# A dilated convolution on one core: nine rows of a store split over 124 and 4 partitions, and the semaphores cleared before the last transfer has landed

## The chip, the cores and the metric

The kernel runs on one core of one Trainium2 chip. The metric is device time in microseconds (us); several runs of one kernel give a median and a spread. The profile is of one execution, and its times count from the start of that execution's span.

## What is computed

A 3x3 convolution with dilation 2 over 16 images of 64 channels and 64x64 pixels, to 128 output channels, in float32 at both ends. `x_pad` is the image with two zeros on every side:

```python
for b in range(batch):
    for co in range(c_out):
        for ci in range(c_in):
            for kh in range(k):
                for kw in range(k):
                    output[b, co] += weight[co, ci, kh, kw] * x_pad[b, ci, kh*dilation:kh*dilation+h, kw*dilation:kw*dilation+w]
```

The input is 16 x 64 x 64 x 64 x 4 B = 16.8 MB, the output twice that, 33.6 MB.

## The kernel before

The images are worked in 8 pairs. A pair's input lies on 128 partitions (two images of 64 channels), its output on 128 partitions (the output channels) with the two images one after the other along the row: `osb[pb % 3]` has 2 x 4096 float32 in each partition. A pair is cut in four groups of 16 rows (`GR = 16`, `NG = 4`), so there are 32 groups `G`.

For each group ScalarE casts input rows to float16 (line 204), VectorE forms sums of row pairs (line 267), TensorE runs three chains of matmuls (line 224), ScalarE copies the shared product out of PSUM (line 210), and VectorE adds it to the two others into `osb` (line 285). Each of these engines runs its own list in group order and waits on counters (`Count`, a semaphore with its running total).

All transfers are issued by SyncE (SP) on one queue, in an order written out by hand: the weights (line 92), four pairs of input (line 98, called from `load`), and then, pair by pair, a wait for the last add of that pair (`done`, line 299), the stores of its two images (`store`, line 301, which issues at line 303) and, while there are any, loads of later pairs. A transfer adds 16 to its semaphore when it is complete; all stores of pair `pb` count on `s_store[pb]`.

The last pair (`pb = 7`) is stored by halves (lines 331 to 335): when its second group is done, rows 0 to 31 of both images go out; when its fourth is done, rows 32 to 63 of both. Each of these four transfers is 128 partitions x 8192 B (32 rows x 64 columns x 4 B). They are the last four transfers of the program.

GpSimd (POOL) has nothing to do after the start but the end: it waits until every `s_store[pb]` has its full count (line 337) and then clears all semaphores of the kernel with one instruction over their range (line 338). After that come the closing barriers of the program (lines 52 and 369 in the profile).

Of the kernel before, what the change touches and what calls it, by code (L numbers as in the profile page):

```python
# [9 lines left out]
def kernel(  # L10
# [7 lines left out]
    nc = tc.nc  # L18

    B, CI, H, W = x.shape  # L20
# [7 lines left out]
    P = 128  # L28
# [5 lines left out]
    HW = H * W  # L34
    GR = 16
    NG = H // GR
# [6 lines left out]
    OF = 3  # L43
# [6 lines left out]
    out_img = out.rearrange("b o h w -> b o (h w)")  # L50

    ctx.enter_context(tc.tile_critical())  # L52
    pe, act, dve, pool, sp = nc.tensor, nc.scalar, nc.vector, nc.gpsimd, nc.sync

    def sb(name, cols, dt):
        return nc.alloc_sbuf_tensor(name, [P, cols], dt).ap()

    x32 = [sb(f"x32_{i}", HW, f32) for i in range(XF)]
    osb = [sb(f"osb_{i}", 2 * HW, f32) for i in range(OF)]
# [24 lines left out]
    sems = []  # L84
# [2 lines left out]
    s_first, s_sum, s_addA, s_addB = map(Count, ("s_first", "s_sum", "s_addA", "s_addB"))  # L87
    s_load = [Count(f"s_load{pb}") for pb in range(npairs)]
    s_store = [Count(f"s_store{pb}") for pb in range(npairs)]


    s_w.by(sp.dma_start(out=w32, in_=weight.rearrange("o i h w -> o (i h w)")), 16)
# [12 lines left out]
    for pb in range(1, XF):  # L105
# [9 lines left out]
            out=ident,  # L115
            in_=ident,
# [156 lines left out]
    for G in range(ngroups):  # L273
        pb, g = divmod(G, NG)
# [7 lines left out]
        for e, c in ((0, s_addA), (1, s_addB)):  # L282
# [3 lines left out]
                    out=o[:, :, b0 : b0 + NBLK, e],  # L286
# [11 lines left out]
    def done(G):  # L298
        sp.wait_ge(s_addB.s, G + 1)

    def store(pb, m, r0=0, r1=H):
        s_store[pb].by(
            sp.dma_start(
                out=out_img[2 * pb + m, :, r0 * W : r1 * W],
                in_=osb[pb % OF][:, m * HW + r0 * W : m * HW + r1 * W],
            ),
            16,
        )

    def store_both(pb, r0, r1):  # L310
        s_store[pb].by(
# [6 lines left out]

    done(NG - 2)
    store(0, 0, 0, (NG - 1) * GR)  # L320
    store(0, 1, 0, (NG - 1) * GR)
    done(NG - 1)
    store_both(0, (NG - 1) * GR, H)
    more(XF)
    for pb in range(1, npairs - 1):
        if pb + XF < npairs:
            more(pb + XF, (0, H) if pb < 2 else (0, H // 2, H))
        done(NG * pb + NG - 1)
        store(pb, 0)
        store(pb, 1)  # L330
    pb = npairs - 1
    for g in (1, NG - 1):
        done(NG * pb + g)
        store(pb, 0, (g - 1) * GR, (g + 1) * GR)
        store(pb, 1, (g - 1) * GR, (g + 1) * GR)
    for pb in range(npairs):
        pool.wait_ge(s_store[pb].s, s_store[pb].n)
    nc.clear_and_free_semaphores(sems)


# [33 lines left out]
```

## Time and profile before

| | |
|---|---|
| time, median of 3 runs | 129.51 us (128.9 to 129.54) |
| profiled execution, its own time | 128.65 us |
| span of the profiled execution | 126.9 us |
| PE / DVE / ACT / POOL busy, share of the span | 82% / 72% / 51% / 2% |
| packets of the one queue that SP fills (q1), share of 16 engines' span | 95.2% |
| moved | 50.66 MB, mean 399 GB/s |
| HBM read / written | 17.07 MB / 33.55 MB |

The profile lists, for each compute engine, how long it was busy; for the transfers, how much of the 16 DMA engines' time was taken by packets. A packet is one contiguous piece that a DMA engine moves; in this kernel it is the part of one partition's row that a transfer names, or 4 B that count up a semaphore. "Landing" is the moment at which the last of a transfer's increments arrived. A slice in the page's rows of digits is 126.9 / 40 = 3.17 us.

### The profile page before, as it was taken

Reading aid. Unit: us, or ns where it says so; the run is one execution under the profiler, and the core shown is the slowest. Engines: PE = TensorE matmul, PEld = TensorE weight load, DVE = VectorE, ACT = ScalarE, POOL = GpSimd, SP = SyncE. Lnnn points to the kernel's source line nnn. Section 1 sums busy time; section 2 is a strip of 40 time slices with the busy share of each in tenths; the row PEclk is TensorE's granted clock in tenths of the full one; section 3 lists DMA queues with packets and bytes.
Section 4 is the critical chain, followed back from the end, with each engine's and each line's share of the span. In section 5 each row is a group of like instructions: output and inputs, shape, how many; then the busy total and the mean of one; then the engine's idle time right before and its main releaser. Section 6 shows DMA issues by size and latency. Waiting matters only on the chain. (4 is left out here: it accounts for less than half of the span.)

```text
span 126.9 us, 2394 instructions
## 1 busy us (share of the span) xinstructions
PE 104.5 (82%) x1000; PEld 56.6 (45%) x1000; DVE 91.0 (72%) x103; ACT 64.9 (51%) x68; POOL 2.2 (2%) x8
## 2 busy tenths in 40 slices
PE   5849999999999999999999999998999999200000
PEld 2325555555555565555555655553555555000000
DVE  0656888988898888888888988878889887600000
ACT  4366566656665666566656665665466633000000
POOL 2400000000000000000000000000000000000000
PEclk9999999999999999999999999999999999995555
DMA  4999999899999999999999999999999999999930
GB/s 111 375 445 439 424 424 403 320 435 403 444 438 444 413 413 434 418 424 449 416 439 416 449 421 413 447 439 429 413 424 444 444 413 418 449 405 426 429 165 15
DMA packets 4595, 50.66 MB, mean 399 GB/s; under 512 B 496, under 2 KB 496, under 8 KB 1008
## 3 DMA queue, kind: packets, MB, share of 16 engines
q1 hardware_dynamic: 4592, 50.63, 95.2%
q8 instruction: 1, 0.02, 0.0%
q14 instruction: 2, 0.02, 0.0%
HBM read 17.07 MB, written 33.55 MB: 399 GB/s over the span
## 5 line engine op out<-in xcount | busy, mean ns | idle before, releaser
L285 DVE TENSOR_TENSOR osb<-ps,psb 128x1024 f32<-128x1024 f32 x64 | 76.8, 1223 | 13.7 <-PE ps L224 12.5
L224 PE MATMUL ps<-x,w_sb 64*128 64x496 f16 (+3 forms) x768 | 84.4, 365 | 0.6 <-PEq L242 0.6
L224 PEld LDWEIGHTS ps<-x,w_sb 64*128 64x128 f16 x768 | 43.7, 94 | 36.5 <-issue 2.3
L210 ACT COPY psb<-ps 128x1024 f32<-128x1024 f32 x32 | 32.4, 1013 | 37.5 <-PE ps L224 37.5
L204 ACT CAST x<-x 128x1024 f16<-128x1024 f32 (+2 forms) x31 | 32.4, 1046 | 0.0
L224 PE MATMUL ps<-xs,w_sb 64*128 64x496 f16 (+1 forms) x192 | 26.0, 371 | 1.6 <-PEq L242 1.6
L224 PEld LDWEIGHTS ps<-xs,w_sb 64*128 64x128 f16 x192 | 10.9, 94 | 10.3 <-issue 1.9
L267 DVE TENSOR_TENSOR xs<-x 128x512 f16<-128x512 f16 x32 | 13.3, 416 | 0.7 <-ACT x L204 0.7
L133 PE MATMUL ps<-zero 128*128 128x512 f16 x10 | 4.1, 533 | 1.4 <-DVE zero L169 1.4
L171 DVE CAST wd<-w 128x192 f16<-128x192 f32 x1 | 0.5, 503 | 2.6 <-DMA w<-in_weight_dram 2.6
L133 PEld LDWEIGHTS ps<-zero 128*128 128x128 f16 x10 | 1.0, 122 | 2.8 <-DVE zero L169 1.4
L144 PEld LDWEIGHTS ps<-ident,wd 128*64 128x64 f16 x30 | 1.0, 109 | 1.9 <-issue 1.5
L144 PE MATMUL ps<-ident,wd 128*64 128x128 f16 x30 | 1.4, 223 | 0.4 <-DVE wd L171 0.4
L183 ACT ACT_TABLE_LOAD x1 | 1.3, 1283 | 0.9 <-SPq L52 0.9
L183 ACT CAST wd<-w 128x192 f16<-128x192 f32 x1 | 0.5, 542 | 1.7 <-DMA w<-in_weight_dram 1.7
L175 DVE CAST w_sb<-ps 128x384 f16<-128x384 f32 x2 | 1.1, 550 | 0.4 <-PE ps L144 0.4
L185 ACT CAST w_sb<-ps 128x384 f16<-128x384 f32 x1 | 0.5, 480 | 1.3 <-PE ps L144 1.3
L169 DVE MEMSET zero<- 128x256 uint32 x1 | 0.3, 272 | 1.1 <-SPq L52 1.1
L188 ACT CAST x<-x 128x512 f16<-128x512 f32 x1 | 0.6, 620 | 0.8 <-DMA x<-in_x_dram 0.8
L177 DVE CAST x<-x 128x640 f16<-128x640 f32 x1 | 0.5, 493 | 0.5 <-DMA x<-in_x_dram 0.5
L125 POOL TENSOR_TENSOR wd<-w 128x192 f16<-128x192 f32 x1 | 0.8, 794 | 2.3 <-DMA w<-in_weight_dram 2.3
L126 POOL CAST wd<-w 128x192 f16<-128x192 f32 x1 | 0.8, 808 | 0.0
(9 smaller groups left out, 2.7 us busy)
## 6 DMA issues: line engine op xcount, KB each, us to landing
out_dram<-osb SPq DMA_DIRECT2D x12, 2048.0 KB, 19.7
x<-in_x_dram SPq DMA_DIRECT2D x5, 2048.0 KB, 18.3
out_dram<-osb SPq DMA_DIRECT2D x5, 1024.0 KB, 13.9
x<-in_x_dram SPq DMA_DIRECT2D x4, 1024.0 KB, 21.5
out_dram<-osb SPq DMA_DIRECT2D x2, 1536.0 KB, 12.4
x<-in_x_dram SPq DMA_DIRECT2D x1, 1088.0 KB, 5.7
x<-in_x_dram SPq DMA_DIRECT2D x1, 960.0 KB, 7.5
w<-in_weight_dram SPq DMA_DIRECT2D x1, 288.0 KB, 2.9
```

Of the source, the lines that this page charges most:

```text
L125: s_pool.by(pool.tensor_tensor(out=wdv[:, 3], in0=wv[:, 0], in1=wv[:, 1], op=sub))
L126: s_pool.by(pool.tensor_copy(out=wdv[:, 4], in_=wv[:, 2]))
L133: pe.matmul(out=dm[:, 0:512], lhsT=zero[:, 0:P], rhs=zero)
L144: m = pe.matmul(out=ps[r * CI : (r + 1) * CI, j * CO : (j + 1) * CO], lhsT=wd[:, t * CI : (t + 1) * CI], rhs=ident,)
L175: dve.tensor_copy(out=turned(k)[0], in_=turned(k)[1])
L183: s_wda.by(act.copy(out=wdv[:, 2], in_=wv[:, 0]))
L188: cast_n[0] = s_act.by(act.copy(out=x16[:, 0 : 8 * W], in_=x32[0][:, 0 : 8 * W]))
L204: act.copy(out=x16[:, lo * W : hi * W], in_=x32[pb % XF][:, lo * W : hi * W])
L210: copy_n[G] = s_act.by(act.copy(out=psb[G % PF], in_=slot(G, 0)))
L224: m = pe.matmul(out=po, lhsT=w_sb[pp, t * CO : (t + 1) * CO], rhs=rhs, start=first and j == 1, stop=last and j == 2,)
L267: s_sum.by(dve.tensor_tensor(out=s, in0=v[:, :, 0], in1=v[:, :, 1], op=add))
L285: dve.tensor_tensor(out=o[:, :, b0 : b0 + NBLK, e], in0=slot(G, 1 + e).rearrange("p (m b q) -> p m b q", m=2, q=2 * W), in1=pv, op=add,)
```

## The change

Three things are changed, all at the end of the kernel.

The store of the first half (rows 0 to 31) of the last image was one transfer of 128 partitions x 8192 B. It becomes three: rows 0 to 22 over 128 partitions (5888 B in each), rows 23 to 31 over partitions 0 to 123 (2304 B in each), and the same nine rows over partitions 124 to 127 (2304 B in each).

The very last store (rows 32 to 63 of the last image) counts on a semaphore of its own, `s_last`. POOL waits for the other stores and for SP's having issued everything (`s_issued`), clears all semaphores but `s_last`, and only then waits for `s_last`.

The instruction that waits for `s_last` also takes its count back to zero, so that no clearing comes after it.

```diff
+    s_issued = Count("s_issued")
+    s_last = Count("s_last")
...
-    def store(pb, m, r0=0, r1=H):
-        s_store[pb].by(
-            sp.dma_start(
-                out=out_img[2 * pb + m, :, r0 * W : r1 * W],
-                in_=osb[pb % OF][:, m * HW + r0 * W : m * HW + r1 * W],
-            ),
-            16,
-        )
+    def store(pb, m, r0=0, r1=H, rows=((0, P),), c=None):
+        for lo, hi in rows:
+            (c or s_store[pb]).by(
+                sp.dma_start(
+                    out=out_img[2 * pb + m, lo:hi, r0 * W : r1 * W],
+                    in_=osb[pb % OF][lo:hi, m * HW + r0 * W : m * HW + r1 * W],
+                ),
+                16,
+            )
...
-    for g in (1, NG - 1):
-        done(NG * pb + g)
-        store(pb, 0, (g - 1) * GR, (g + 1) * GR)
-        store(pb, 1, (g - 1) * GR, (g + 1) * GR)
+    FOUR = ((0, P - 4), (P - 4, P))
+    ROWS4 = 9
+    done(NG * pb + 1)
+    store(pb, 0, 0, 2 * GR)
+    store(pb, 1, 0, 2 * GR - ROWS4)
+    store(pb, 1, 2 * GR - ROWS4, 2 * GR, FOUR)
+    done(NG * pb + NG - 1)
+    store(pb, 0, 2 * GR, H)
+    store(pb, 1, 2 * GR, H, c=s_last)
+    sp.sem_inc(s_issued.s, 1)
+
+
+    pool.wait_ge(s_issued.s, 1)
     for pb in range(npairs):
         pool.wait_ge(s_store[pb].s, s_store[pb].n)
-    nc.clear_and_free_semaphores(sems)
+    nc.clear_and_free_semaphores(sems[:-1])
+    pool.wait_ge(s_last.s, s_last.n).then_inc(s_last.s, -s_last.n)
+    nc.release_semaphore(s_last.s)
```

## The prediction

> **What bounds the kernel now.** I read the page's rows by slices first, then the chain that ended last, then the transfers from 109 us on, then POOL's last instructions.
>
> The rows by slices (40 slices of 3.17 us; the digit is a busy share in tenths):
>
> ```profile
> PE   5849999999999999999999999998999999200000
> DVE  0656888988898888888888988878889887600000
> DMA  4999999899999999999999999999999999999930
> ```
>
> The 16 DMA engines are full from the second slice on. Compute stops five slices before the end. The chain of waits, in order of time, ends with VectorE:
>
> ```profile
> 107.54 2.36 DVE osb L285 x2
> ```
>
> That is 109.90 us; the span is 126.88. What follows is no engine's work: the stores still queued. SP issues the last two at once:
>
> ```profile
> 109.92 1.48 SPq L303 DMA_DIRECT2D out_dram<-osb  x2
> ```
>
> The transfers between 109 and 127 us (40 slices of 0.45 us):
>
> ```profile
> DMA  9959968999899999999999999996311111000000
> GB/s 583 401 255 510 583 255 364 419 437 455 364 473 419 419 437 419 401 455 419 419 437 437 419 419 437 400 473 255 127 55 55 55 55 55 18 18 0 0 0 0
> ```
>
> This row carries the prediction. About 420 GB/s until some 121.5 us, then 55, then 18, then nothing. Stretches, with the DMA share and GB/s as the last two numbers:
>
> ```profile
> 118.00:120.00 2.00, 0.00 (x0) 0.00 (x0) 0.00 (x0) 0.00 (x0) 0.00 (x0) 0.50 1.02 430
> 122.70:124.40 1.70, 0.00 (x0) 0.00 (x0) 0.00 (x0) 0.00 (x0) 0.00 (x0) 0.50 0.11 48
> 124.46:125.10 0.64, 0.00 (x0) 0.00 (x0) 0.00 (x0) 0.00 (x0) 0.00 (x0) 0.50 0.06 26
> ```
>
> With all at work 430 / 16 = 26.9 GB/s each; alone, one moves 26. So a DMA engine's pace is its own and doesn't rise when the others stop. And 26 GB/s is one engine: two of the sixteen work alone at the end, then one. In the trace's packet records the last increments of fourteen engines go out between 121.34 and 122.24 us, of the other two at 124.45 and 125.13. **The end is set by two late DMA engines**, up to 125.13 - 122.24 = 2.89 us behind the last of the rest. Each had the same bytes: all transfers here have 128 partitions, 8 for each engine.
>
> Then POOL (durations min/median/max in ns, then first and last start):
>
> ```profile
> L338 POOLq DRAIN  x1: 105/105/105, 125.7 to 125.7; - x1
> L338 POOLq EVENT_SEMAPHORE_RANGE_CLEAR  x1: 200/200/200, 125.8 to 125.8; - x1
> L52 POOLq DRAIN  x1: 34/34/34, 126.1 to 126.1; - x1
> ```
>
> The last increment lands at 125.57 (15.3 us after the issue at 110.30), 0.45 after its packet. In the records POOL's wait follows at 125.598, the drain at 125.684, the clearing at 125.819, the closing drain at 126.068; the span ends at 126.88.
>
> **Part 1, the nine rows.** They are 9 x 64 x 4 = 2304 B in each partition. Before, they were part of a packet of 8192 B, 8 packets per engine. In the packet records consecutive packets start 306 ns apart at 8192 B, 156 at 4096 (stores), 288 at 7680 and 90 at 2304 (the weights); 8192 and 2304 make 36.7 ps per byte and 5.5 ns per packet, so 5888 B take 221 ns.
>
> For twelve engines: 8 x (306 - 221) = 0.68 us less, if they have no share of the nine rows. For those that take them: how a transfer of 124 partitions is divided no row shows. All traced transfers give every engine equal shares; 124 doesn't divide by 16, and the largest count up to 16 that divides both 124 and 4 is four. So I take four engines with 31 packets from one transfer and 1 from the other. Such an engine: 8 x 221 + 32 x 90 + 2 increments of 6 = 4.66 us, against 8 x 306 = 2.45: 2.21 us more. The bounds: packets 86 ns each by the pace alone (2304 / 26.8; 0.13 us less in all), or slower from sharing (rival 2); shares of one sixteenth (nothing changes) or all on four.
>
> If the four are among the fourteen, they finish between 121.34 + 2.21 = 123.55 and 122.24 + 2.21 = 124.45. The late ones finish at 123.77 and 125.13 - 0.68 = 124.45. So the late one still ends, or is level: **0.68 us gained**, and no more rows would help.
>
> The Trainium skill, "DMA: Bandwidth & Descriptors", section "Why a DMA increments its semaphore by 16 and not by 1", says that the number of engines is the largest up to 16 that divides the slowest dimension, and that SP's queue uses the lowest-numbered; "Latency and other measured facts" there calls engines 7 and 15 usually the slower ones. Together they would make the four miss the late ones. The trace's two late engines fit this; which numbers they have no record here shows.
>
> SP issues two transfers more. Its issues took 0.33 to 1.11 us; after the pair at 103.6 to 105.05 it waits until 109.92, so 2 x 1.11 fits in its 4.9 us. If it didn't, the last pair would be issued later, with engines that have work until 114.3 and beyond (the first landing of the pair issued at 103.6). Cost nothing.
>
> **Part 2, the clearing.** Drain and clearing go from behind the last landing to before it: the closing drain can start where the drain did, 126.068 - 125.684 = **0.38 us gained**. Bounds: 0.31 if the closing drain then takes the other's 105 ns instead of 34, 0.40 if the wait is faster (17 instead of 43 ns). Cover: POOL now waits for the last store but one, which an engine ends 2.45 us before its last, and the clearing needs some 0.5; uncovered it would cost those 0.38 back. SP's signal comes with its last issue, 111.4 us in this trace, 11 us before it is needed. Behind POOL's new wait stands only the closing drain. The decrement is in the waiting instruction; a wait with a decrement took 17 ns in the closing barrier.
>
> **Sum.** 0.68 + 0.38 = 1.06 us. Against the profiled execution: 128.65 - 1.06 = 127.59. The median of the runs shown is 0.86 above that execution, so the prediction is 129.51 - 1.06 = 128.45, 0.8% faster. An unprofiled lag may differ; that the runs are longer than the profiled one speaks against a smaller one, since the other fourteen had no idle time to lose.
>
> **Rivals.** *1: the move relieves nobody.* The nine rows may be shared out nearly evenly after all, or the late engine's pace may hang on the partitions it reads and not on the engine, so that others that read them take its time away. Then only the clearing counts: 129.51 - 0.38 = 129.13, no change that a measurement of this kernel can tell (0.5%, 0.65 us). For it: no traced transfer lets an engine read another's partitions. Against it: the pace stayed at 26 GB/s with one engine alone.
>
> *2: the four become the end, slower than before.* The place is their 32 packets. They have 124.45 + x against 125.13 + 0.38 of the old end, so it is slower from x = 1.06 us for the last of them, 33 ns on each packet (from 1.96 us, 61 ns, if the four are the earliest). If a packet takes twice as long, because it meets another engine that reads the same partitions, x = 32 x 90 = 2.88: the end is at 126.43 to 127.33, 1.30 to 2.20 later, less 0.38 gives 130.43 to 131.33. If one of the two late engines is among the four, it ends at 124.45 + 2.21 or 125.13 + 2.21, which with the 0.38 gives 130.66 to 131.34. For it: the first 2304 B packets of the weights took up to 642 ns while all began at once. Against: later ones held 93.
>
> A rule speaks for this rival: the skill's "SBUF — State Buffer", section "Door 1: The DMA port swizzle", has 16 ports, each for eight fixed partitions, and DMA speed limited by the ports reached. By it 31 neighbouring partitions read by one engine use ports that are already full, and the sum would be near rival 2 instead of -1.06. No row of before can show it.
>
> **How the numbers follow.** If any four of the sixteen are as likely, they miss both late ones with 12/16 x 11/15 = 0.55. I give the forecast 0.56 and divide the rest evenly: rival 1 0.22, rival 2 0.22. The forecast's own range is 127.7 (lowest run 128.9 less 1.06, rounded down) to 128.8 (less 0.68, where the lag is 0.4 short). Over 0.5% faster: 0.56, within: 0.22, slower: 0.22. The range goes from 127.6 to the near end of rival 2, 130.4; what lies beyond has under 0.2.
>
> **What would show it.** In the profile after: the tail at 48 to 55 GB/s replaced by about 100 to 160 (four to six engines), ending near 124.5 instead of 125.1; landing of the last transfer near 124.9; 31 packets of 2304 B on each of four engines, 90 ns apart; POOL's clearing near 123 and the closing drain some 0.1 us after the last landing. Packets of 2304 B well over 93 ns, or four engines that end after 125.1, would be rival 2; a tail as before, rival 1. The prediction is wrong if the late engines of the timed runs are others, or less late.

## The result, and the profile after

| | before | after |
|---|---|---|
| median of 19 runs | 128.78 us (128.12 to 130.22) | 127.71 us (127.40 to 129.44) |
| profiled execution / its span | 128.65 / 126.9 us | 127.42 / 125.6 us |
| last landing in that profile | 125.57 us | 124.71 us |
| from there to the end of the span | 1.31 us | 0.93 us |

The ratio after to before is 0.9927, 95% interval 0.9904 to 0.9949: 0.94 us faster, by the interval 0.66 to 1.24. The three runs of before that the prediction was made against lay high: their median was 129.51, that of 19 runs is 128.78.

The page of the kernel after, first its span, then the row of the DMA engines by slices of 3.14 us, then SP's queue (packets, MB, share of 16 engines' span):

```profile
span 125.6 us, 2398 instructions
...
DMA  3999999899999999999999999999999999999971
...
q1 hardware_dynamic: 4728, 50.63, 96.4%
```

The row ends in 71 instead of 30: the engines now stop more nearly together. There are 136 packets more than before: 128 of 2304 B and 8 increments. The transfers from 109 to 127 us, in slices of 0.45 us as for before:

```profile
DMA  9798989999999999999999998966444320000000
GB/s 510 328 546 364 473 346 382 401 455 419 400 411 394 431 395 467 395 428 449 418 415 462 392 497 364 492 291 255 200 182 200 146 109 36 0 0 0 0 0 0
```

The 55 and 18 GB/s of two engines and then one have become about 200, some seven engines (the four with the nine rows and, in this execution, three late ones), and 36 in the last slice. The drop from full speed comes half a slice to a slice earlier and the end earlier too: the rest is spread over more engines.

POOL's last instructions (durations in ns, then first and last start):

```profile
L350 POOLq DRAIN  x1: 105/105/105, 122.4 to 122.4; - x1
L350 POOLq EVENT_SEMAPHORE_RANGE_CLEAR  x1: 201/201/201, 122.5 to 122.5; - x1
```
```profile
L351 POOLq EVENT_SEMAPHORE  x1: 17/17/17, 124.7 to 124.7; - x1
```
```profile
L52 POOLq DRAIN  x1: 34/34/34, 124.8 to 124.8; - x1
```

Drain and clearing are over at 122.71, two microseconds before the last landing. Behind the wait for it (L351) comes the closing drain at once, at 124.83.

SP's four issues of the first halves, in place of two:

```profile
L306 SPq DMA_DIRECT2D out_dram<-osb x4: 332/1061/1112, 103.8 to 106.4; - x4
```

The last of them ends at 107.54 (106.44 + 1.10); SP's next issue is at 110.12, after the last add as before (109.92 there).

In the packet records the pieces of 2304 B follow each other every 90 ns on four engines (each took 93 ns and overlaps the next by 3), those of 5888 B every 221. The landings of the very last transfer are 121.32 to 122.14 for nine engines, then 123.51, 123.86, 124.12, 124.21, 124.33, 124.57 and 124.71. Which is which follows from the second transfer of the pair before, whose parts landed at 111.87 to 113.03, and late at 114.35, 115.06 and 115.20. From there an engine without the nine rows has 24 packets of 8192 B, 8 of 5888 and four increments: 24 x 0.306 + 8 x 0.221 + 4 x 0.006 = 9.14 us. So the late ones land at 123.49, 124.20 and 124.34 (found: 123.51, 124.21, 124.33). With 32 x 0.090 + 2 x 0.006 more, 12.03 us, the four are the ones at 123.86, 124.12, 124.57 and 124.71 (from 111.87, 112.14, 112.57 and 112.71: 123.90, 124.17, 124.60, 124.74). In this execution **the four end last, 0.38 us behind the late ones.**

The last landing is 0.86 us earlier than in before's profile, but not all of that is the change. The latest part of the pair before had landed at 115.20 here and at 115.79 there, so the late engine was 0.59 us less late to begin with. With the store in one, 32 packets of 8192 B and four increments follow: 32 x 0.306 + 4 x 0.006 = 9.82 us, which gives before's last landing to 0.04 (115.79 + 9.82 = 125.61, found 125.57). Here it would have been 115.20 + 9.82 = 125.02, so by this estimate the nine rows took 0.31 us off the last landing in this execution.

### The profile page after: what moved, and what is told of

It is laid out like the page before. It is cut to its first block, busy times and chain, and to the rows that moved or that the text cites. A ratio compares the mean times of both kernels' runs of the same rounds, so it can differ in the third digit from the quotient of the medians.

```text
span 125.6 us, 2398 instructions
## 1 busy us (share of the span) xinstructions
PE 104.5 (83%) x1000; PEld 55.9 (44%) x1000; DVE 91.0 (72%) x103; ACT 64.9 (52%) x68; POOL 2.2 (2%) x8
## 5 line engine op out<-in xcount | busy, mean ns | idle before, releaser
L226 PEld LDWEIGHTS ps<-x,w_sb 64*128 64x128 f16 x768 | 43.2, 94 | 36.8 <-issue 2.1
```

The source lines that it names most:

```text
L226: m = pe.matmul(out=po, lhsT=w_sb[pp, t * CO : (t + 1) * CO], rhs=rhs, start=first and j == 1, stop=last and j == 2,)
```

## The experiments

All are edits of the kernel after, or of before where it says so; ratios are to before, and 0.01 is 1.29 us.

**The two parts alone.** First the nine rows with the old end:

```diff
...
-    store(pb, 1, 2 * GR, H, c=s_last)
-    sp.sem_inc(s_issued.s, 1)
+    store(pb, 1, 2 * GR, H)
...
-    pool.wait_ge(s_issued.s, 1)
...
-    nc.clear_and_free_semaphores(sems[:-1])
-    pool.wait_ge(s_last.s, s_last.n).then_inc(s_last.s, -s_last.n)
-    nc.release_semaphore(s_last.s)
+    nc.clear_and_free_semaphores(sems)
```

> The nine rows over 124 and 4 partitions alone; the clearing stays behind the last landing as before. If the late DMA engines are relieved by 8 packets of 85 ns, the last transfer lands 0.6 to 0.7 us earlier and the kernel is that much faster, about -0.65 us. If the move relieves nobody, no change. If the clearing alone made the gain, no change either. The two parts are independent if this and the clearing alone add up to the whole change (about -0.94 us by the ratio 0.9927).

Measured: 0.9933 (0.9907 to 0.9959), 0.86 us faster, by the interval 0.53 to 1.20. The transfers from 109 to 127 us in its profile:

```profile
DMA  7998989899999998999999999955433312000000
GB/s 328 473 510 364 401 364 492 364 419 419 435 399 402 444 444 362 463 410 433 438 410 431 410 419 401 401 219 218 182 164 164 164 73 91 18 0 0 0 0 0
```

The last landing is at 125.32, and the span ends 1.31 us later, as before. In this execution the latest engine was later: its part of the pair before landed at 116.23. With the store in one it would have landed 9.82 us on, at 126.05; with the rows moved it is 9.14, 125.37. So by this estimate the move took 0.73 us off, and here the late engine ends last, at 18 GB/s, with the four done by 124.80 (112.81 + 12.03 = 124.84 for the last of them). The move relieves the late engines. Then the earlier clearing with the store in one:

```diff
-    store(pb, 1, 0, 2 * GR - ROWS4)
-    store(pb, 1, 2 * GR - ROWS4, 2 * GR, FOUR)
+    store(pb, 1, 0, 2 * GR)
```

> The earlier clearing alone; the store of the first half stays one transfer. From the last landing to the end of the span 1.31 us before and 0.93 in the changed kernel, so -0.38 us here (ratio 0.997) and the last landing where it was. If the gain of the change is all in the clearing, -0.9 us.

Measured: 0.9959 (0.9928 to 0.9989), 0.53 us faster, by the interval 0.14 to 0.93; the expected 0.38 lies in it. In its profile the last landing is at 125.52 (before: 125.57), and the wait's instruction and the closing drain follow at 125.54 and 125.64. The transfers from 109 to 127 us still end with two engines and one:

```profile
DMA  9969996999999999999998999995311010000000
GB/s 510 510 291 437 473 382 273 473 401 455 419 437 419 455 400 473 401 437 437 382 492 346 437 419 437 419 455 219 146 55 73 36 73 18 36 0 0 0 0 0
```

So both parts bring something. Whether either alone is the whole can't be told by time: 0.53 to 1.20 and 0.14 to 0.93 both overlap the 0.66 to 1.24 of the change. The profiles show that each does its own part: with the rows alone the 1.31 us behind the last landing are back, with the clearing alone the last landing is where it was.

**The same pieces, over all engines.**

```diff
-    store(pb, 1, 2 * GR - ROWS4, 2 * GR, FOUR)
+    store(pb, 1, 2 * GR - ROWS4, 2 * GR)
```

> As the changed kernel, but the nine rows are one transfer over all 128 partitions, so every engine has 8 packets of 2304 B and the bytes are even again. If what helps is which engines take the nine rows, this is the clearing alone, -0.35 us, with two late engines alone at the end. If cutting the store into smaller pieces helps by itself, it is as fast as the changed kernel, -0.94 us.

Measured: 0.9983 (0.9953 to 1.0013), 0.2 us faster, which can't be told from none; the clearing's 0.38 lies in the interval, the 0.94 of the change doesn't. Its tail is that of before, down to the single engine's 18 GB/s:

```profile
DMA  9969977997999998999999998989321111000000
GB/s 473 437 291 546 473 328 328 473 437 309 505 397 436 395 423 355 498 405 463 403 387 494 374 509 346 492 346 382 127 91 73 73 55 55 18 0 0 0 0 0
```

Cutting the store up isn't what helps; which engines move the pieces is.

**Seven engines.** An attempt to spread more rows over more engines:

```diff
-    FOUR = ((0, P - 4), (P - 4, P))
-    ROWS4 = 9
+    FOUR = ((0, 119), (119, 126), (126, P))
+    ROWS4 = 16
```

> As the changed kernel, but sixteen rows instead of nine, over 119, 7 and 2 partitions. If a transfer goes to as many engines as the largest count up to 16 that divides its partitions, always the first ones, the sixteen rows (4096 B, 156 ns) go to seven engines with 17 or 18 packets (one or two engines 19) instead of 8. Those seven end 1.4 to 1.6 us later than before, at 122.9 to 123.8; the late ones have 8 x 150 = 1.2 us less and end near 123.9 instead of 125.1: -1.2 us from the transfers and -0.38 from the clearing, -1.6 us in all. If the seven include a late engine, that one ends near 126 and the kernel is slower than before by 0.5 us or more. If engines that read others' partitions are slowed, packets of 4096 B take well over 159 ns.

Measured: 1.0179 (1.0128 to 1.0230), slower by 2.3 us. One engine alone ends at 128.2, more than three microseconds after the others (a stretch of that time; DMA share and GB/s are the last numbers):

```profile
125.80:128.20 2.40, 0.00 (x0) 0.00 (x0) 0.00 (x0) 0.00 (x0) 0.00 (x0) 0.50 0.06 24
```

A late engine is among the seven. And packets were stretched, which the changed kernel didn't show: of the pieces of 4096 B, 159 ns alone, sixteen took 13 to 632 ns longer, the last two of these (632 and 329 ns, at 121.01 and 121.87) at a time when only the late engine can still have had pieces. 18 or 19 pieces more (2.8 to 3.0 us), 8 packets shorter by 150 ns (1.2 us less) and those 0.96 us make 2.6 to 2.8 of the 3.1 us by which it ends later than the last one of before (128.2 against 125.1).

**Eighteen rows.**

```diff
-    ROWS4 = 9
+    ROWS4 = 18
```

> As the changed kernel with eighteen rows instead of nine over 124 and 4 partitions. 18 rows are 4608 B, 175 ns a packet at the changed kernel's pace; the four engines have 32 of them and 8 packets of 3584 B (137 ns) in place of 8 of 8192 B: 6.7 us instead of 2.45, 4.2 us more. They end near 126.4 and the last landing is near 126.8, 1.3 us later than before; with the clearing's -0.38 the kernel is about 0.9 us slower than before (ratio 1.007). If engines that read other engines' partitions also slow each other, the packets take well over 175 ns and it is slower still. If the nine rows helped in another way than by the balance of bytes, eighteen help as much or more: -0.9 us or better.

Measured: 1.0201 (1.0123 to 1.0280), slower by 2.6 us where 0.9 was expected; the last landing is at 127.85 instead of 126.8. In the packet records 18 of the 128 pieces of 4608 B took 11 to 391 ns longer than the 178 ns of the others, 3.6 us in all, and 18 packets of 8192 B another 1.7 us. The tail falls in long steps, four engines that end one after the other:

```profile
DMA  9999969999999999999899997434343333222120
GB/s 510 400 437 401 510 291 401 419 400 455 388 413 395 428 465 386 456 386 482 351 411 379 412 353 270 165 137 181 142 174 146 164 127 127 109 91 109 73 91 36
```

So there is a point from which the four are the end, and beyond it a second price: packets that take longer. What lengthens them isn't shown.

**Which engines are late.** The kernel before, with row 63 of the second image of two pairs in pieces, each with a semaphore of its own:

```diff
+    PIECES = {5: (4, 5, 6, 7, 8, 9, 10, 15, 64), 6: (11, 12, 13, 14, 14, 64)}
...
         store(pb, 0)
-        store(pb, 1)
+        if pb in PIECES:
+            store(pb, 1, 0, H - 1)
+            lo = 0
+            for n in PIECES[pb]:
+                marker(pb, lo, lo + n)
+                lo += n
+        else:
+            store(pb, 1)
```

> The kernel before, with row 63 of the second image of the sixth and seventh pair stored in pieces of 4, 5, 6, 7, 8, 9, 10, 15 and of 11, 12, 13, 14 partitions, each with its own semaphore; nothing is left out. Each engine does its queue in order, so an engine that is 2 to 3 us late lands its part of each piece 2 to 3 us late. If a piece of n partitions goes to the first n engines, always the same ones, the number of late landings in a piece of n tells how many late engines are among the first n: 0 for 4 by the changed kernel, 1 for 7 by the run with seven engines (its last landing was 3.4 us behind the others). If late engines are the eighth and the last, as the notes on the chip would have it, there is none up to 7 and one from 8 to 15. The time itself is of no interest here; some us more are expected from twelve small issues.

The increments of each piece, by time in us. Here are four of the pieces. One update comes as SP's issue ends, 10 to 15 us before the others (left of the bar), and then there is one for each engine:

```
 4:  86.70 | 101.98 102.17 102.61 103.02
 5:  87.58 | 102.18 102.35 102.79 103.21 105.68
11: 100.41 | 111.80 111.96 111.97 112.19 112.37 112.39 112.57 112.66 113.11 113.58 116.37
12: 101.54 | 111.99 112.14 112.15 112.40 112.58 112.61 112.76 112.84 113.30 113.77 115.17 116.57
```

A piece of n partitions lands n times, for each of the n from 4 to 15. From 4 to 5 one landing is added that is 2.5 us late, so **the fifth engine is late**, if a piece of n goes to the first n engines, always the same ones; up to 11 there is no other, and the twelfth adds a second. The first four have none. The counts grow in step, as that premise asks; the records themselves don't name engines.

The same pieces in the changed kernel:

> The changed kernel with the same pieces of row 63 in the sixth and seventh pair as in the pieces run. If the late engines are fixed, the pieces of 4 have no late landing, 5 to 11 have one, 12 to 15 have two, as in the pieces run. If lateness moves about, the counts differ. The time is of no interest.

```
 4:  89.94 | 104.11 104.26 105.13 106.36
 5:  90.72 | 104.31 104.45 105.33 106.54 109.00
12: 103.68 | 114.06 114.22 114.23 114.35 114.62 114.65 114.85 114.86 114.93 115.88 117.06 119.88
13: 104.72 | 114.24 114.41 114.42 114.53 114.83 114.86 115.03 115.07 115.11 116.07 116.13 117.24 120.08
```

Here the fifth is again the latest, but two of the first four are 1 and 2 us behind too; the twelfth is not late, but the thirteenth is, by 1 us. So only half of the expectation holds: one late place is the same in both, the others move between executions.

**Five engines.** The test of that in timed runs:

```diff
-    FOUR = ((0, P - 4), (P - 4, P))
+    FOUR = ((0, P - 3), (P - 3, P))
```

> As the changed kernel, but the nine rows over 125 and 3 partitions: five engines with 25 packets and three of them with one more. By the pieces run the fifth engine is the latest one. Then it has 8 x 221 + 25 x 90 = 4.02 us in place of 2.45, ends 1.57 us later than before, near 126.7, and the kernel is 1.57 - 0.38 = 1.2 us slower than before (ratio 1.009), although four of the engines have fewer packets than in the changed kernel. If which engine is late changes from execution to execution, the timed runs scatter between that and a gain, and the ratio is near that of the changed kernel. If the gain of the change doesn't hang on which engines take the rows, it is as fast as the changed kernel (0.993).

Measured: 1.0105 (1.0060 to 1.0151), 1.35 us slower; the fifth engine with 25 packets instead of none turns the gain into a loss. The last landing is at 126.91, its data end at 126.47 (expected 126.7). No packet of the last pair was stretched, and the tail ends with one engine for two microseconds:

```profile
DMA  9989979999999999999999999944342300000000
GB/s 473 473 364 437 473 328 401 382 419 492 400 376 426 403 439 429 433 417 438 410 455 409 432 426 444 408 190 184 127 200 109 127 36 36 36 18 36 18 18 0
```
```profile
124.30:126.40 2.10, 0.00 (x0) 0.00 (x0) 0.00 (x0) 0.00 (x0) 0.00 (x0) 0.50 0.06 27
```

**Seven rows,** since the four ended last in the profile after:

```diff
-    ROWS4 = 9
+    ROWS4 = 7
```

> As the changed kernel with seven rows instead of nine over 124 and 4 partitions. In the profile of the changed kernel the four engines land last, at 124.71, the late ones at 124.33. Two rows less are 19 ns less per packet: the four end 24 x 0.019 = 0.45 us earlier (124.26), the late ones 8 x 0.019 = 0.15 later (124.48), so the kernel is 0.2 us faster than the changed one and 1.2 us faster than before (ratio 0.991). If the late engines end last in the timed runs, it is 0.15 us slower than the changed kernel instead. Both are near what the rounds can tell.

Measured: 0.9926 (0.9887 to 0.9965). With it, on the same chip, the changed kernel once more:

> The changed kernel once more, on the chip of the run with seven rows. 0.993 of before, as measured first; with the interval of the single parts (0.9933 for the rows, 0.9959 for the clearing) their product 0.989 would also be possible.

Measured: 0.9916 (0.9877 to 0.9955). Seven and nine rows can't be told apart by these runs. In the profile of each the four end last: at 124.92 with seven rows (two of their pieces were stretched, by 30 and 212 ns) with the late one at 124.82, and at 124.69 against 124.40 with nine. None of the kernels tried is measurably faster than the changed one.

**Eighteen rows in two lots,** to see what stretches the packets:

```diff
-    store(pb, 1, 0, 2 * GR - ROWS4)
+    store(pb, 1, 0, 2 * GR - 2 * ROWS4)
+    store(pb, 1, 2 * GR - 2 * ROWS4, 2 * GR - ROWS4, FOUR)
     store(pb, 1, 2 * GR - ROWS4, 2 * GR, FOUR)
```

> The eighteen rows of the earlier run, in two lots of nine: four engines have 64 packets of 2304 B instead of 32 of 4608 B, the same bytes. At 90 ns each they end 8 x 137 + 64 x 90 - 2448 = 4.4 us later than before, the last landing is near 127.0 and the kernel 1.1 us slower than before (ratio 1.008). If the stretched packets of the eighteen-row run (up to 392 ns over) came from the size of the packets, there are none here and the ratio is 1.008; if they come from how long four engines read partitions that others read too, packets of 2304 B are stretched as well and the ratio is again near 1.02.

Measured: 1.0115 (1.0058 to 1.0173), 1.5 us slower, nearer to 1.008 but with the other value just outside the interval. The profile speaks against the size alone: 11 pieces of 2304 B too took up to 406 ns longer, and of the 384 packets of 8192 B 125 took up to 1384 ns longer, 20.5 us in all where the eighteen rows in one lot had 1.7. It also shows something new in the eight issues of SP from 105.8 us on:

```profile
L306 SPq DMA_DIRECT2D out_dram<-osb x8: 332/1091/3947, 105.8 to 115.8; - x8
```

One issue, the second lot's 4 partitions, took 3.95 us, and so the last two stores were issued at 114.8 and 115.8 instead of 109.9 and 110.3. What stretches the packets stays open: reading partitions that another engine reads, and writing to memory, were not separated.

## Why the prediction was right, point by point

- **The bound.** Two late DMA engines set the end of before: shown, by the rows alone (0.9933, and 0.73 us of the last landing in their profile). That the same pieces over all engines leave the tail as it was (0.9983) excludes the cutting as the cause.
- **Four engines take 124 and 4 partitions:** right. The four increments of the piece of 4, and the 32 packets of 2304 B on each of four engines, show it. The prediction took this from equal shares; the Trainium skill's "DMA: Bandwidth & Descriptors", section "Why a DMA increments its semaphore by 16 and not by 1", states it, and these runs agree for 4 to 15 engines and for 119, 124 and 125 partitions (7, 4 and 5 engines).
- **They miss the late ones:** right in the three profiles of these nine rows over four engines without pieces, though not in every execution: with the pieces two of the first four were late. The prediction could only count (0.55) and set a rule beside it: the Trainium skill's same page, section "Latency and other measured facts", calls engines 7 and 15 usually slower, with a guessed cause that it calls specific to transfers issued through GpSimd; here SP issues them all. These runs don't show that pattern: the fifth in order is late in both runs with pieces, the twelfth in one, the thirteenth in the other; neither the eighth (from 7 to 8 partitions) nor the sixteenth (from 15 to 64) adds a late landing; and transfers over five or seven engines lose (1.0105, 1.0179). That a transfer takes the first ones, always the same, fits all of them. So the rule adds nothing to the count of 0.55, and that a late engine is the fifth and not one of the first four was in part luck.
- **Prices:** 90 and 221 ns a packet, as predicted. The four's price agrees with the landings above to 0.05. Two slips in the working: the clearing's upper bound, 0.384 + 0.026, is 0.41 and not 0.40, and the lowest run less the sum, 128.9 - 1.06, is 127.84 and not 127.7. The sum uses neither.
- **0.68 us from the rows:** the rows alone gave 0.86 (0.53 to 1.20). Predicted was that the late one still ends last, or level, near 124.9. So it was in the profile of the rows alone (125.32 against 124.80 for the four). In the profile after it was not: the late ones landed at 124.33 and the four at 124.71, so this step was off by 0.38 us there, and by 0.29 in the second profile of the changed kernel (124.40 and 124.69). The reason is the lag, the time from the landing of the latest of the four to that of the latest engine, at the pair before. The move makes the four 2.21 us later and the late one 0.68 earlier, so by the prediction's own prices it takes off 0.68 or the lag less 2.21, whichever is less. The lags were 3.42 us with the rows alone (116.23 - 112.81), 2.49 after (115.20 - 112.71) and 2.57 in its second profile (115.25 - 112.68). That gives 0.68, 0.28 and 0.36, where the landings with 9.82 us for the store in one give 0.73, 0.31 and 0.38. The sum was made from one profile, whose lag was at least 3.03 us (115.79 against at most 112.76); the prediction did say that another lag may differ, but put nothing in the sum for it. "No more rows would help" holds: 7 and 9 can't be told apart, 18 lose.
- **0.38 us from the clearing:** 1.31 us after the last landing became 0.93, exactly the term of the sum; timed alone 0.53 (0.14 to 0.93).
- **Costs put at nothing:** SP's two issues (1.11 and 1.10 us) fit into its wait. The cover of the clearing was 2.0 us.
- **Rival 1** (the move relieves nobody) is excluded by the first and third experiment. **Rival 2** (the four become the end, slower than before) did not come true at nine rows, where the four end last but before the old end. It exists: it is what happened with 18 rows and, in its second form, with five engines, where the late engine itself got more (1.35 us slower, by the prediction's way of reckoning 1.2). Its stretched packets came with 16 and 18 rows; in all five profiles with nine rows over four or five engines every piece of them took 93 ns, and with seven rows two pieces were stretched, by 30 and 212 ns. The rule on the 16 ports of "SBUF — State Buffer", section "Door 1: The DMA port swizzle", speaks for a slowing at nine rows as well; the 93 ns are against it there, and for the larger moves these runs don't tell whether the ports are the cause.
- **The number:** predicted 128.45, measured 127.71. The difference of 0.74 is that of the base, 129.51 against 128.78 (0.73), and it put the measured time close to the low end of the range (127.6); that it stayed inside owes something to luck. The predicted step of 1.06 stands against 0.94 (0.66 to 1.24) by the ratio and 1.07 by the medians.

## What to carry to other kernels

When the compute engines have stopped and only stores run, look at the GB/s of the last slices: 18 or 55 instead of 430 meant here that one or two DMA engines were behind, and that they should get fewer bytes than the others. In these runs a transfer's number of partitions chose how many engines carry it, always from the first on, so find out with small pieces which engines are late before choosing, and in more than one execution: 124 and 4 partitions or 125 and 3 was the difference between 0.7% faster and 1% slower. What can be done before the last landing (a clearing, a signal) should not stand behind it.

## What the runs showed of the hardware that was not expected

- One engine is late from early on. In every profile one packet of another queue (q8, instructions, 16 KB) took 954 to 987 ns at 11.6 to 13.9 us, and in all but one the load that landed next had one more part behind the rest (before: 15.13 us against 14.27 for the one ahead of it). But in the changed kernel's profile one part was late already in the first load of images (7.43 us against 6.66), and in that of the changed kernel with the pieces, the exception, three were (7.59, 7.64 and 8.74 against 6.61). What makes an engine late stays open.
- The late engines other than the fifth differ from execution to execution: in the changed kernel's profile three were late (by 1.3 to 2.2 us at the pair before the last), in before's two; with the pieces, two of the first four.
- A transfer over few engines can hold up SP for 3.3 to 3.9 us when much is queued (in the changed kernel with the pieces, and in the eighteen rows in two lots); in the profile of the changed kernel its longest issue of a store was 1.11 us.
